# Splitting the operands of the scan's C-times-state product into three fp32r matmuls

## The chip, the cores and the metric

The kernel runs as one program on one core of a Trainium2 chip. The metric is device time in microseconds (us) of one execution, as the median of several runs; lower is better. The core's engines have queues of their own and run side by side: PE multiplies matrices, DVE, ACT and POOL do elementwise work, and DMA transfers are issued from the queues of SP and ACT. On every queue the instructions go in order: an instruction that waits holds back all that stand behind it.

## The reference, cut to what matters

One layer of an encoder with 1024 tokens and a width of 1024. Its input projection feeds a windowed attention branch and a state-space (SSD) branch, which are merged; a cross-attention and an MLP with 4096 hidden columns follow. The change lies in the SSD branch: 8 groups of 4 heads, a state of 128 rows per head column, 8 chunks of 128 tokens, and a scan in both directions.

```python
CB = jnp.einsum('bclgn,bcsgn->bcgls', Cc, Bc)
Wd = CB[:, :, :, None] * segsum_exp(adt)
y_diag = jnp.einsum('bcgrls,bcsgrp->bclgrp', Wd, xdt)
states = jnp.einsum('bcsgn,bcgrs,bcsgrp->bcgrpn', Bc, decay_states, xdt)
...
_, prev = lax.scan(step, init, (jnp.moveaxis(states, 1, 0), jnp.moveaxis(chunk_decay, 1, 0)))
y_off = jnp.einsum('bclgn,bcgrpn,bcgrl->bclgrp', Cc, prev, jnp.exp(a_cs))
...
y = y_fwd + y_bwd + d_skip.astype(f32)[:, None] * xs
y = y.reshape(b, l, D_INNER) * jax.nn.silu(z.astype(f32))
yg = yg * lax.rsqrt(jnp.mean(yg * yg, axis=-1, keepdims=True) + EPS)
```

All inputs and outputs are fp32.

## The kernel before, in words

Most matrix products are made from split operands: a high part `hi` that is the fp32 value copied to the type fp32r, and a low part `lo`, which is the value minus `hi`. `mm3` then issues three fp32r matmuls (hi by hi, hi by lo, lo by hi) into one accumulator. Splitting takes one copy on ACT and one subtraction on POOL (for weights, `split_in`, lines 64 and 67) or on DVE. The scan itself has some products in plain fp32.

`ssd_phase` is a list of jobs. For each group there is a job for each of four convolved inputs (`conv_job`, named `cps` in the profile), one for a block of gate logits (`gate_job`, `gps`) and one for z (`z_job`, `zp`). A job yields after each unit of three matmuls, and `at` says after which unit a piece of scan work is put in. PE runs in exactly this written order. For the other engines a scheduler sets the order of each queue when the program is built. The order of a group is: `conv_job` 0 and 1, `gate_job`, `conv_job` 2 and 3, `z_job`. The scan steps of the group before go into the first four of these, two to a job (after units 8 and 16), from chunk 7 down to 0; in each job a unit is three matmuls of 512 columns. The last group's steps go into three more gate jobs, closer together.

The names to follow:

- `state(q, c)`, in the z job, makes the states of chunk c in three fp32r products (`st`, lines 551 to 553) and puts the running states into `prev` (128 by 8 chunks by 2 directions by 256).
- `back(q, c)` on POOL adds the backward direction's decayed state into `prev`.
- `prep(q, c)` loads two rows of cumulated decay by DMA (`rows`, issued on ACT's queue, line 573), masks them on POOL (lines 574 and 576) and takes their exponentials on ACT, one for each of four heads and two directions (`ef`, `eb`, lines 583 and 584); DVE adds the two (line 585).
- `mask(q, c)` makes the product of C and B (`cb`, line 590), with which DVE multiplies `ef` (line 592).
- `step(q, c)` makes the in-chunk product (`cb`, line 606, four heads of 64 columns) and the product of C with the states (`yo`, line 610, plain fp32, 512 columns, or 256 for chunks 0 and 7). DVE scales `yo` into `t` (line 614), POOL makes the skip term `p1` and adds the backward half to it (lines 621, 623), and DVE adds up `y` and multiplies it by the gate factors `zs` (lines 628 to 630). ACT squares it and sums it (line 631). After every fourth chunk `scale_rows` takes the inverse root on POOL (`rr`, line 122) and scales the four rows on ACT (line 642); `yt` turns them on PE and stores them.
- A `conv_post` follows each convolution job: ACT reads the accumulator (line 413), DVE adds four shifted products (lines 417 and 419), ACT takes a tanh (`th`, line 421), DVE finishes (line 422).

Buffers come from named rings: `wop` has 6 buffers of weights, which is three pairs; `raw` 2; `rows` 2; `ef` 3. The z job uses two pairs of weights: one from `wop` and one in tiles of its own, `z0` and `z1`.

Of the kernel before, what the change touches and what calls it, by code (L numbers as in the profile page):

```python
# [7 lines left out]
F32 = mybir.dt.float32  # L8
F32R = mybir.dt.float32r
I32 = mybir.dt.int32  # L10
AF = mybir.ActivationFunctionType
ALU = mybir.AluOpType
# [4 lines left out]
P = 128  # L17
S = 1024
D = 1024
NT = 8  # L20
# [37 lines left out]
def split_in(kx, src, hi, lo, eng=None, pin=False):  # L58

    nc = kx.nc  # L60
    n = hi.shape[-1]
    raw = kx.wp.tile([P, 1024], F32, tag="raw", bufs=kx.raw_bufs, name="raw")[:, :n]
    nc.sync.dma_start(raw, src)
    steps = [nc.scalar.activation(hi, raw, AF.Copy)]  # L64
    if pin:
        kx.tc.keep_in_program_order(steps[0])
    steps.append((eng or nc.gpsimd).tensor_tensor(lo, raw, hi.bitcast(F32), ALU.subtract))  # L67
    if pin:
        kx.tc.keep_in_program_order(steps[1])


def wload(kx, src, n=1024, hi=None, lo=None, eng=None, pin=False):
    if hi is None:
        hi = kx.wp.tile([P, 1024], F32R, tag="wop", bufs=6, name="whi")[:, :n]
        lo = kx.wp.tile([P, 1024], F32R, tag="wop", bufs=6, name="wlo")[:, :n]
    split_in(kx, src, hi, lo, eng, pin)
    return hi, lo
# [372 lines left out]
def ssd_phase(kx, ins, dr):  # L450


    nc, tc = kx.nc, kx.tc
    V, A, G, PE = nc.vector, nc.scalar, nc.gpsimd, nc.tensor
    with tc.tile_pool(name="p1", bufs=1) as sp, tc.manual_schedule(engines={mybir.EngineType.PE}):
# [31 lines left out]

        def z_job(q):
            def load():
                zhl = [sp.tile([P, 1024], F32R, tag=f"z{i}", bufs=1, name=f"z{i}") for i in range(2)]  # L490
                return [wload(kx, ins["wssd"][q.g, 4], hi=zhl[0], lo=zhl[1]), wload(kx, ins["wssd"][q.g, 5])]

            def run(zw):
                zws = wsplit(zw[0], 4) + wsplit(zw[1], 4)
                q.zt = []
                q.zs = sp.tile([P, NT, 256], F32, tag="zs", bufs=1, name="zs")
                for b in range(3, -1, -1):
                    zp = kx.pp.tile([P, 512], F32, tag="p", name="zp")
                    for j in range(2):
                        t = 2 * b + j  # L500
                        for k in range(NK):
                            mm3(kx, zp[:, j * 256:(j + 1) * 256],
                                act_pair(kx.hT[t // 4], k, slice((t % 4) * P, (t % 4) * P + P)),
                                zws[k], k == 0, k == NK - 1)
                            yield
                    zb = q.zs[:, 2 * b:2 * b + 2].rearrange("p c q -> p (c q)")
                    q.zt.append(A.activation(zb, zp, AF.Tanh, scale=0.5))
                    V.scalar_tensor_tensor(zb, zb, 1.0, zp, ALU.add, ALU.mult)
            return load, run
# [77 lines left out]
        def mask(q, c):  # L587
# [3 lines left out]
            ef = q.efs[c]  # L591
            V.tensor_tensor(ef, ef, cb[:, :P].unsqueeze(1).broadcast_to([P, 4, P]), ALU.mult)

        def step(q, c):

            b, j = c // 4, c % 4
            cl = slice(c * P, (c + 1) * P)
            cb, ef = q.cb, q.efs[c]
            if c:
                mask(q, c - 1)  # L600
            if c > 1:
                prep(q, c - 2)
            if j == 3:
                q.yz, q.ss = [None] * 4, sp.tile([P, 4], F32, tag="ss", bufs=2, name="ss")
            for h in range(4):
                PE.matmul(cb[:, 256 + 64 * h:256 + 64 * h + 64], ef[:, h], q.xtok[:, c, 64 * h:64 * h + 64],  # L606
                          start=True, stop=True)
            lo, hi = (256 if c == 0 else 0), (256 if c == NT - 1 else 512)
            yo = kx.pp.tile([P, 512], F32, tag="p", name="yo")
            PE.matmul(yo[:, lo:hi], q.CT[:, cl], q.prev[:, c].rearrange("p d q -> p (d q)")[:, lo:hi],  # L610
                      start=True, stop=True)
            d0, d1 = lo // 256, hi // 256
            t = sp.tile([P, 2, 256], F32, tag="t", bufs=1, name="t")
            V.tensor_tensor(t[:, d0:d1].rearrange("p d (h q) -> p d h q", h=4),
                            yo[:, lo:hi].rearrange("p (d h q) -> p d h q", h=4, q=64),
                            kx.ecs[:, b, j, d0:d1, q.hs].unsqueeze(3).broadcast_to([P, d1 - d0, 4, 64]), ALU.mult)
            single = q.g == NG - 1 and b == 0
            if single and j == 0:
                scale_rows(q, 1, 3)
            p1 = sp.tile([P, 256], F32, tag="p1", bufs=2, name="p1")  # L620
            G.tensor_tensor(heads(p1), heads(q.xtok[:, c]), dsk[:, q.hs].unsqueeze(2).broadcast_to([P, 4, 64]), ALU.mult)
            if d1 - d0 == 2:
                G.tensor_tensor(p1, p1, t[:, 1], ALU.add)
            if c > 1:
                with tc.issue_after(q.shut.ins):
                    back(q, c - 1)
            y = q.yz[j] = sp.tile([P, 256], F32, tag="yz", bufs=8, name="yz")
            V.tensor_tensor(y, cb[:, 256:], t[:, d0], ALU.add)
            V.tensor_tensor(y, y, p1, ALU.add)
            V.tensor_tensor(y, y, q.zs[:, c], ALU.mult)  # L630
            A.activation(q.zs[:, c], y, AF.Square, accum_out=q.ss[:, j:j + 1])
            if single and j == 0:
                scale_rows(q, 0, 1)
                q.done = b, q.yz
            elif not single and j == 0:
                scale_rows(q, 0, 4)
                q.done = b, q.yz
# [21 lines left out]
        for g in range(NG):  # L659
            q, o = gs[g], gs[g - 1]  # L660
            scan = lambda *cs: [(step, o, c) for c in cs] if g else []
            if g == 0:
                job(conv_job(q, 3), {8: [(tm_x, q)]})
            else:
                job(conv_job(q, 0), {8: [(step, o, 7)], 16: [(step, o, 6)]})
                job(conv_job(q, 1), {8: [(step, o, 5)], 16: [(step, o, 4)]})
                job(gate_job(g), {8: [(step, o, 3)], 16: [(step, o, 2)]})
                job(conv_job(q, 2), {8: [(step, o, 1)], 16: [(yt, o), (step, o, 0)]})
                job(conv_job(q, 3), {8: [(tm_x, q)], 16: [(yt, o)]})
            first = 17 if g else 24  # L670
            at = {first + (63 - first) * c // 7: [(state, q, c)] for c in range(NT)}
            at[4] = [(tm_b, q)]
            at.setdefault(58, []).append((prep, q, 7))
            at[64] = [(prep, q, 6), (mask, q, 7)]
            job(z_job(q), at)
        q = gs[7]
        job(gate_job(8), {5: [(step, q, 7)], 10: [(step, q, 6)], 15: [(step, q, 5)]})
# [3 lines left out]
        for n, ((_, run), at) in enumerate(jobs):  # L681
            nxt = jobs[n + 1][0][0]() if n + 1 < len(jobs) else None
            i = 0
# [1206 lines left out]
```

## Time and profile before

| | us |
|---|---|
| median of 3 runs | 2308.64 (2307.11 to 2309.57) |
| the profiled execution, its own time | 2306.48 |
| its span, first to last instruction | 2304.7 |
| PE busy | 2288.2 (99%) |
| DVE busy | 1582.1 (69%) |
| ACT busy | 1173.3 (51%) |
| POOL busy | 935.3 (41%) |
| the SSD phase with scan steps, from about 126 to 900: PE busy of 774 | 772.6 |

Rows of the profile give the source line, the engine, the operation, the tile written and the tiles read. Matmul durations in the groups contain the way through the array, and overlap; the chain of waits shows how long each holds PE. Times are from the start of the span. The 774 us of the scan hold 7 periods of about 101.8 us, one for each group, that look alike; the period whose steps start at 655 us serves as the example.

### The profile page before, as it was taken

How to read it: one execution, taken by the hardware profiler on the slowest of the kernel's cores; microseconds unless marked ns; L12 is line 12 of the kernel's file. 1: busy time of each engine (PE TensorE's matmuls, PEld its weight loads, DVE VectorE, ACT ScalarE, POOL GpSimd, SP SyncE). 2: the span in 40 equal slices, each digit the busy share in tenths (PEclk: the TensorE clock that was granted, in tenths of full speed). 3: DMA queues.
4: the chain of work that ended last, by engine and by line, in shares of the span. 5: the costliest groups of instructions: out<-in, count | busy, mean ns of one | idle time of the engine just before them, and what ended most of it. 6: DMA issues, size and time to landing. Idle time of an engine off the chain costs nothing.

```text
span 2304.7 us, 32485 instructions
## 1 busy us (share of the span) xinstructions
PE 2288.2 (99%) x11882; PEld 1941.3 (84%) x11882; DVE 1582.1 (69%) x2501; ACT 1173.3 (51%) x2486; POOL 935.3 (41%) x885
## 2 busy tenths in 40 slices
PE   9999999999999999999999999999999999999998
PEld 8888898989888897888888888888988887888887
DVE  5877666677766673467659887866685456489984
ACT  5454655555565555488865442346563334233341
POOL 2355647555564745355540021125585454100010
PEclk9999999999999999999999999999999999999999
DMA  6222323233232323111145257112453345712201
GB/s 235 83 83 92 110 74 110 83 101 91 93 102 74 119 74 110 40 44 35 51 153 183 92 184 255 45 37 65 138 177 129 118 152 183 274 74 108 103 28 74
DMA packets 150754, 252.09 MB, mean 109 GB/s; under 512 B 11457, under 2 KB 86337, under 8 KB 150594
## 3 DMA queue, kind: packets, MB, share of 16 engines
q1 hardware_dynamic: 79840, 211.46, 27.1%
q10 hardware_dynamic: 70754, 38.55, 5.9%
q8 instruction: 94, 1.54, 0.3%
q14 instruction: 66, 0.54, 0.1%
HBM read 202.25 MB, written 47.71 MB: 108 GB/s over the span
## 4 chain that ended last, share of the span: by engine, by line
PE 88%; DVE 4%; ACT 2%; DMA 2%; issue 1%; POOL 1%; ACTq 0%; SPq 0%; POOLq 0%; DVEq 0%
PE mps L1630 10%; PE dps L1630 10%; PE pb L1416 6%; PE cps L83 4%; PE cps L88 4%; PE cps L87 4%; PE pc L1416 3%; PE zp L83 2%; PE zp L88 2%; PE zp L87 2%; PE cb L606 2%; PE yo L610 2%; PE gps L83 2%; PE gps L88 2%; PE gps L87 2%; PE mps L87 1%
## 5 line engine op out<-in xcount | busy, mean ns | idle before, releaser
L67 POOL TENSOR_TENSOR wlo<-raw,whi 128x1024 fp32r<-128x1024 f32 x96 | 235.5, 2453 | 385.3 <-ACT whi L64 374.1
L1581 ACT ACTIVATE kt<-row 128x512 fp32r<-128x512 f32 x264 | 143.8, 619 | 183.6 <-PE dps L1630 82.9
L1630 PE MATMUL mps<-kt 128*128 128x512 f32 x1008 | 229.8, 389 | 0.0
L1630 PE MATMUL dps<-kt 128*128 128x512 f32 x1008 | 228.6, 389 | 0.0
L1630 PEld LDWEIGHTS dps<-kt 128*128 128x128 f32 x1008 | 189.2, 188 | 39.3
L1630 PEld LDWEIGHTS mps<-kt 128*128 128x128 f32 x1008 | 188.9, 188 | 39.4 <-DVE kt L1582 0.3
L83 PE MATMUL cps<-kt,whi 128*128 128x512 f32 x512 | 215.2, 420 | 0.0
L88 PE MATMUL cps<-kt,wlo 128*128 128x512 f32 x512 | 200.0, 391 | 0.0
L87 PE MATMUL cps<-kt,whi 128*128 128x512 f32 x512 | 199.3, 389 | 0.0
L64 ACT ACTIVATE whi<-raw 128x1024 fp32r<-128x1024 f32 x104 | 109.6, 1055 | 149.1 <-DMA raw<-in_wa_dram 27.4
L1582 DVE TENSOR_TENSOR kt<-row,kt 128x512 fp32r<-128x512 f32 x264 | 171.5, 697 | 1.5 <-ACT kt L1581 1.4
L548 POOL TENSOR_TENSOR xl<-xs,xh 128x512 fp32r<-128x512 f32 (+1 forms) x64 | 85.9, 1343 | 105.4 <-ACT xh L547 80.7
L122 POOL TENSOR_TENSOR rr<-rv,mhalf 128x1 f32<-128x1 f32 (+2 forms) x50 | 34.6, 694 | 226.1 <-DVE rv L120 224.3
L1361 POOL TENSOR_TENSOR wop<-w,wop 128x512 fp32r<-128x512 f32 x64 | 87.1, 1363 | 82.6 <-ACT wop L1360 79.1
L87 PEld LDWEIGHTS cps<-kt,whi 128*128 128x128 f32 x512 | 96.3, 188 | 25.3 <-issue 6.7
L83 PEld LDWEIGHTS cps<-kt,whi 128*128 128x128 f32 x512 | 96.2, 188 | 24.9 <-issue 5.5
L88 PEld LDWEIGHTS cps<-kt,wlo 128*128 128x128 f32 x512 | 96.1, 188 | 20.8
L583 ACT ACTIVATE ef<-rows,ebias 128x128 f32<-128x128 f32 x256 | 91.2, 394 | 34.4 <-PE cb L606 30.8
L808 DVE CUSTOM_DVE_ANT_0 t<-sps,bias,snk 128x384 f32<-128x384 f32 (+1 forms) x128 | 71.4, 581 | 52.3 <-PE sps L807 51.7
L816 POOL TENSOR_SCALAR t<-t,den 128x384 f32<-128x384 f32 (+1 forms) x128 | 69.2, 560 | 90.3 <-DVE den L814 81.2
L584 ACT ACTIVATE eb<-rows,ebias 128x128 f32<-128x128 f32 x256 | 89.9, 394 | 30.2 <-POOL rows L576 30.1
L1299 POOL TENSOR_TENSOR wd<-row,wd 128x1024 fp32r<-128x1024 f32 x4 | 11.1, 2794 | 228.4 <-ACT wd L1298 228.4
(392 smaller groups left out, 6576.7 us busy)
## 6 DMA issues: line engine op xcount, KB each, us to landing
rows<-d_cs ACTq DMA_DIRECT2D x128, 256.0 KB, 3.8
raw<-in_wssd_dram SPq DMA_DIRECT2D x48, 512.0 KB, 3.8
raw<-in_wup_dram SPq DMA_DIRECT2D x41, 512.0 KB, 4.2
d_u<-c SPq DMA_DIRECT2D x64, 256.0 KB, 3.0
row<-in_wdn_dram SPq DMA_DIRECT2D x28, 512.0 KB, 6.4
row<-d_u SPq DMA_DIRECT2D x28, 512.0 KB, 6.2
x<-in_x_dram SPq DMA_DIRECT2D x16, 512.0 KB, 6.6
raw<-in_wg_dram SPq DMA_DIRECT2D x16, 512.0 KB, 3.7
```

Source lines behind the costliest of these rows:

```text
L64: steps = [nc.scalar.activation(hi, raw, AF.Copy)]
L67: steps.append((eng or nc.gpsimd).tensor_tensor(lo, raw, hi.bitcast(F32), ALU.subtract))
L83: i = mm(out, l[0], r[0], start=first, stop=False)
L87: mm(out, l[0], r[1], start=False, stop=False)
L88: mm(out, l[1], r[0], start=False, stop=last)
L583: A.activation(ef[:, h], rows[:, 0, h], AF.Exp, bias=kx.ebias[:, b, j, 0, o:o + 1])
L584: A.activation(eb[:, h], rows[:, 1, h], AF.Exp, bias=kx.ebias[:, b, j, 1, o:o + 1])
L1361: self.kx.nc.gpsimd.tensor_tensor(t[:, 1], src, t[:, 0].bitcast(F32), ALU.subtract)
L1416: self.kx.nc.tensor.matmul(ps, w[:, i, ks], act[:, k, j], start=start and k == 0 and m == 0, stop=k == 3 and m == 2, skip_group_check=True)
L1581: nc.scalar.activation(t[:, j, 0], src, AF.Copy)
L1582: nc.vector.tensor_tensor(t[:, j, 1], src, t[:, j, 0].bitcast(F32), ALU.subtract)
L1630: self.kx.nc.tensor.matmul(ps[t], lt[:, k, x, ts], rt[:, k, y], start=n in (1, 2, 5) and k == 0 and m == 0, stop=k == 3 and m == 2, skip_g ...
```

## The change

1. `step` makes `yo` from three fp32r products of split operands in the place of one fp32 product. C is split once for each group (`split_c`: one ACT copy, one DVE subtraction of 128x1024, after unit 52 of the z job). The states of a chunk are split just before they are used (`split_prev`: one ACT copy to `prh`, one DVE subtraction to `prl`, 128x512, or 128x256 for chunks 0 and 7). The pair has one buffer. The split for chunk c-1 is written into step c, behind the scaling of `yo`, and the block `issue_after` puts the subtraction behind that scaling in DVE's queue; it adds no wait to ACT's copy.
2. The product with the gate factors is written over them (`zs[:, c]`), and the squares go to `y`, which now has 2 buffers; the 8 buffers of `yz` are gone.
3. The z job takes both pairs of weights from the common ring `wop`, which still has three pairs; `z0` and `z1` are gone.

```diff
         def z_job(q):
             def load():
-                zhl = [sp.tile([P, 1024], F32R, tag=f"z{i}", bufs=1, name=f"z{i}") for i in range(2)]
-                return [wload(kx, ins["wssd"][q.g, 4], hi=zhl[0], lo=zhl[1]), wload(kx, ins["wssd"][q.g, 5])]
+                return [wload(kx, ins["wssd"][q.g, i]) for i in (4, 5)]
...
+        def split_c(q):
+            q.chl = [sp.tile([P, S], F32R, tag=n, bufs=1, name=n) for n in ("ch", "cl")]
+            A.activation(q.chl[0], q.CT, AF.Copy)
+            V.tensor_tensor(q.chl[1], q.CT, q.chl[0].bitcast(F32), ALU.subtract)
+
+        def split_prev(q, c):
+            lo, hi = (256 if c == 0 else 0), (256 if c == NT - 1 else 512)
+            q.pair = [sp.tile([P, 512], F32R, tag=n, bufs=1, name=n) for n in ("prh", "prl")]
+            ph, pl = (t[:, lo:hi] for t in q.pair)
+            pv = q.prev[:, c].rearrange("p d q -> p (d q)")[:, lo:hi]
+            A.activation(ph, pv, AF.Copy)
+            V.tensor_tensor(pl, pv, ph.bitcast(F32), ALU.subtract)
...
-            PE.matmul(yo[:, lo:hi], q.CT[:, cl], q.prev[:, c].rearrange("p d q -> p (d q)")[:, lo:hi],
-                      start=True, stop=True)
+            ph, pl = (t[:, lo:hi] for t in q.pair)
+            PE.matmul(yo[:, lo:hi], q.chl[0][:, cl], pl, start=True, stop=False)
+            PE.matmul(yo[:, lo:hi], q.chl[0][:, cl], ph, start=False, stop=False)
+            PE.matmul(yo[:, lo:hi], q.chl[1][:, cl], ph, start=False, stop=True)
...
+            if c:
+                with tc.issue_after(scaled.ins):
+                    split_prev(q, c - 1)
...
-            y = q.yz[j] = sp.tile([P, 256], F32, tag="yz", bufs=8, name="yz")
+            y = sp.tile([P, 256], F32, tag="y", bufs=2, name="y")
+            yz = q.yz[j] = q.zs[:, c]
...
-            V.tensor_tensor(y, y, q.zs[:, c], ALU.mult)
-            A.activation(q.zs[:, c], y, AF.Square, accum_out=q.ss[:, j:j + 1])
+            V.tensor_tensor(yz, y, yz, ALU.mult)
+            A.activation(y, yz, AF.Square, accum_out=q.ss[:, j:j + 1])
...
+            at.setdefault(52, []).append((split_c, q))
...
-            at[64] = [(prep, q, 6), (mask, q, 7)]
+            at[64] = [(prep, q, 6), (mask, q, 7), (split_prev, q, 7)]
```

The line numbers of the changed kernel are shifted by up to 19 behind the new functions. The next rows are instructions in the order of their queues.

PE, one step of 512 columns between two jobs, before:

```order
L590 MATMUL cb<-cC,cB 128x128
L606 MATMUL cb<-xtok,ef 128x64 x4
L610 MATMUL yo<-prev,cC 128x512
L83 MATMUL cps<-kt,whi 128x512
L87 MATMUL cps<-kt,whi 128x512
```

PE, the same place in the changed kernel:

```order
L589 MATMUL cb<-cC,cB 128x128
L618 MATMUL cb<-xtok,ef 128x64 x4
L623 MATMUL yo<-prl,ch 128x512
L624 MATMUL yo<-prh,ch 128x512
L625 MATMUL yo<-prh,cl 128x512
```

One fp32 matmul became three fp32r ones, and the first of them reads the low part `prl`, which DVE writes last.

ACT, from the reading of the second convolution job's accumulator to the scaling of the first four rows, before. The numbers at the names tell buffers apart: `ef_5977` and `ef_6044` belong to chunks 1 and 0, `rows_6609` to chunk 7 of the next group, `yz_5912` to chunk 4, `rr_5919` is the inverse root of chunks 7 to 4:

```order
L413 ACTIVATE cx_5925<-cps_5784,cols_376 128x1024
L583 ACTIVATE ef_5977<-rows_5968,ebias_175 128x128 x4
L584 ACTIVATE eb_6045<-rows_6035,ebias_175 128x128 x4
L64 ACTIVATE whi_6079<-raw_6081 128x1024
L573 DMA rows_6609<-d_cs_72 128x4x128 x2
L583 ACTIVATE ef_6044<-rows_6035,ebias_175 128x128 x2
L421 ACTIVATE th_5931<-cx_5925 128x1024
L631 ACTIVATE zs_5265,ss_5684<-yz_5912 128x256
L583 ACTIVATE ef_6044<-rows_6035,ebias_175 128x128 x2
L573 DMA rows_6658<-d_cs_72 128x4x128
L642 ACTIVATE yz_5912<-yz_5912,rr_5919 128x256
```

ACT, the same place in the changed kernel. `prh_6142` and `prh_6239` are the high parts of chunks 3 and 2, `ef_6217` and `ef_6290` the exponentials of chunks 1 and 0, `rr_6159` the inverse root of chunks 7 to 4:

```order
L413 ACTIVATE cx_6165<-cps_6012,cols_376 128x1024
L603 ACTIVATE prh_6142<-prev_5503 128x512
L582 ACTIVATE ef_6217<-rows_6208,ebias_175 128x128 x4
L583 ACTIVATE eb_6291<-rows_6281,ebias_175 128x128 x4
L572 DMA rows_6873<-d_cs_72 128x4x128 x2
L649 ACTIVATE y_6152,ss_5900<-zs_5473 128x256
L582 ACTIVATE ef_6290<-rows_6281,ebias_175 128x128 x3
L660 ACTIVATE zs_5473<-zs_5473,rr_6159 128x256 x4
L421 ACTIVATE th_6171<-cx_6165 128x1024
L603 ACTIVATE prh_6239<-prev_5503 128x512
```

The scaling of the four rows, which waits for `rr` from POOL, now stands ahead of the tanh, and the split of chunk 2 behind both.

DVE, the end of the second convolution job's sums, before (`t_5995` is chunk 3's scaled product):

```order
L419 SCALAR_TENSOR_TENSOR cx_5925<-cps_5784,cols_376,cx_5925 128x1022
L630 TENSOR_TENSOR yz_5912<-yz_5912,zs_5265 128x256
L592 TENSOR_TENSOR ef_5887<-ef_5887,cb_5965 128x512
L585 TENSOR_TENSOR ef_5977<-ef_5977,eb_5978 128x512
L422 SCALAR_TENSOR_TENSOR cx_5925<-th_5931,cx_5925 128x1024
L120 TENSOR_SCALAR rv_5917<-ss_5684 128x4
L614 TENSOR_TENSOR t_5995<-yo_5993,ecs_176 128x512
```

DVE, the same place in the changed kernel (`t_6237` is chunk 3's scaled product, `prl_6240` the low part of chunk 2):

```order
L120 TENSOR_SCALAR rv_6157<-ss_5900 128x4
L591 TENSOR_TENSOR ef_6121<-ef_6121,cb_6205 128x512
L419 SCALAR_TENSOR_TENSOR cx_6165<-cps_6012,cols_376,cx_6165 128x1022
L584 TENSOR_TENSOR ef_6217<-ef_6217,eb_6218 128x512
L628 TENSOR_TENSOR t_6237<-yo_6233,ecs_176 128x512
L646 TENSOR_TENSOR y_6249<-cb_6109,t_6237 128x256
L422 SCALAR_TENSOR_TENSOR cx_6165<-th_6171,cx_6165 128x1024
L604 TENSOR_TENSOR prl_6240<-prev_5503,prh_6239 128x512
```

The sum for the inverse root (`rv`) went ahead of the job's last step (L422), and the low part of chunk 2 stands right behind that step.

POOL, the same place in the changed kernel (`wlo_6332` is a weight's low part, `p1_6146` the skip term of chunk 4):

```order
L573 AFFINE_SELECT rows_6281<-rows_6281 128x512
L67 TENSOR_TENSOR wlo_6332<-raw_6333,whi_6331 128x1024
L575 AFFINE_SELECT rows_6281<-rows_6281 128x512
L640 TENSOR_TENSOR p1_6146<-p1_6146,t_6140 128x256
L564 TENSOR_TENSOR cb_t_6318<-prev_5503,dec_177 128x256
L565 TENSOR_TENSOR prev_5503<-prev_5503,cb_t_6318 128x256
L638 TENSOR_TENSOR p1_6315<-xtok_5393,dsk_944 128x256
L573 AFFINE_SELECT rows_6873<-rows_6873 128x512
L122 TENSOR_TENSOR rr_6159<-rv_6157,mhalf_169 128x4
```

The inverse root has one masking of rows for the next group ahead of it; before, both stood ahead of it.

More of the change, by code (lines that the diff above doesn't have):

```diff
@@ L609, in step @@
             yo = kx.pp.tile([P, 512], F32, tag="p", name="yo")
-            PE.matmul(yo[:, lo:hi], q.CT[:, cl], q.prev[:, c].rearrange("p d q -> p (d q)")[:, lo:hi],
-                      start=True, stop=True)
+            ph, pl = (t[:, lo:hi] for t in q.pair)
+            PE.matmul(yo[:, lo:hi], q.chl[0][:, cl], pl, start=True, stop=False)
+            PE.matmul(yo[:, lo:hi], q.chl[0][:, cl], ph, start=False, stop=False)
+            PE.matmul(yo[:, lo:hi], q.chl[1][:, cl], ph, start=False, stop=True)
             d0, d1 = lo // 256, hi // 256
             t = sp.tile([P, 2, 256], F32, tag="t", bufs=1, name="t")
-            V.tensor_tensor(t[:, d0:d1].rearrange("p d (h q) -> p d h q", h=4),
+            scaled = V.tensor_tensor(t[:, d0:d1].rearrange("p d (h q) -> p d h q", h=4),
                             yo[:, lo:hi].rearrange("p (d h q) -> p d h q", h=4, q=64),
                             kx.ecs[:, b, j, d0:d1, q.hs].unsqueeze(3).broadcast_to([P, d1 - d0, 4, 64]), ALU.mult)
+            if c:
+                with tc.issue_after(scaled.ins):
+                    split_prev(q, c - 1)
             single = q.g == NG - 1 and b == 0
```

## The prediction

> **What bounds the kernel now.** I read the page first: busy shares and the chain of work that ended last.
>
> ```profile
> span 2304.7 us, 32485 instructions
> PE 2288.2 (99%) x11882; PEld 1941.3 (84%) x11882; DVE 1582.1 (69%) x2501; ACT 1173.3 (51%) x2486; POOL 935.3 (41%) x885
> PE 88%; DVE 4%; ACT 2%; DMA 2%; issue 1%; POOL 1%; ACTq 0%; SPq 0%; POOLq 0%; DVEq 0%
> ```
>
> PE is the bound: time taken off its queue comes off the end, as long as PE does not wait instead. Next the stretch in which the scan steps run, and in it four successive intervals, each from the end of one `yo` to the end of the next.
>
> ```profile
> 126.00:900.00 774.00, 772.62 (x4480) 667.39 (x4479) 531.63 (x740) 436.53 (x1054) 459.47 (x459) 1.00 0.31 95
> 671.48:678.92 7.44, 7.44 (x38) 6.00 (x37) 7.15 (x10) 4.46 (x11) 5.13 (x7) 1.00 0.45 135
> 678.92:686.36 7.44, 7.44 (x38) 6.00 (x37) 6.33 (x9) 5.59 (x14) 7.04 (x8) 1.00 0.33 102
> 686.36:693.80 7.44, 7.44 (x38) 6.00 (x37) 7.13 (x10) 3.05 (x8) 5.98 (x6) 1.00 0.51 160
> 693.80:701.24 7.44, 7.44 (x38) 6.00 (x37) 3.71 (x8) 3.48 (x9) 5.78 (x6) 1.00 0.48 161
> ```
>
> After each stretch and its length the columns are busy us of PE, weight load, DVE, ACT and POOL. PE waits 1.4 us in all of 774, at a granted clock of 1.00. But DVE is nearly full in the two convolution jobs: 7.15, 6.33 and 7.13 of 7.44, and rests only in the gate job (3.71). That is where a new dependency can turn into a wait.
>
> **The matmuls.** The chain of waits shows what a product holds PE for.
>
> ```profile
> 656.11 0.49 PE yo L610 x2
> 670.57 0.91 PE yo L610 x2
> 692.89 0.91 PE yo L610 x2
> 729.44 0.12 PE st L551
> 731.93 0.23 PE st L551
> 732.16 0.23 PE st L552
> 732.40 0.24 PE st L553
> ```
>
> The fp32 `yo` takes 0.91 us with 512 columns and 0.49 with 256. The states' own fp32r products, three into one accumulator as the changed `yo` will have them, take 0.23 + 0.23 + 0.24 = 0.70 and 3 x 0.12 = 0.36. A step thus saves 0.21 or 0.13. A group has 6 wide and 2 narrow steps: 6 x 0.21 + 2 x 0.13 = 1.52 us; 8 groups give **12.2 us**. No row shows three fp32r products right behind the fp32 `cb`; the 0.69 that three times 0.23 gives would add 0.5 us in all, and I leave it out.
>
> **The splits.** ACT gets 64 copies and 8 of C, DVE as many subtractions. By the nearest rows (ACT's copy of 128x512 and DVE's subtraction to fp32r of that size):
>
> ```profile
> L547 ACT ACTIVATE xh<-xs 128x512 fp32r<-128x512 f32 x6 | 3.8, 628 | 2.6 <-PE zp L88 1.1 <-PE st L552 0.9 <-DVE xs L543 0.6
> L520 DVE TENSOR_TENSOR bl<-tm,bh 128x512 fp32r<-128x512 f32 x2 | 1.3, 674 | 0.0
> L543 DVE TENSOR_TENSOR xs<-xtok,coef 128x512 f32<-128x512 f32 x6 | 7.8, 1297 | 1.8 <-POOL xl L548 1.8
> ```
>
> a wide split is 0.63 on ACT and 0.67 on DVE, up to the 1.30 that DVE's product of two SBUF tiles has in the z job. By themselves they are hidden: PE reads the pair a whole step later. C's split (about twice that, 1.3 and 1.3 us) lies in the z job, 12 units of 3 x 0.12 and 8 of 3 x 0.23 us ahead of the first step, some 10 us; it costs nothing while PE has these matmuls. Its low bound is nothing, its high one 1 us a group, if it holds up a state's split. But DVE gets fuller: the three intervals from 671.48 hold 7.15 + 6.33 + 7.13 = 20.61 us of work, with three subtractions 22.6, in 3 x 7.23 = 21.7 us. The queue falls behind by about 1 us by chunk 2's step and catches up in the gate job. So the question is which step's `prl` comes too late.
>
> **The wait that can come.** The order of the changed queues shows it at one place in each of the seven first groups: chunk 2's pair stands, on ACT, behind the scaling of four rows (which waits for POOL's inverse root) and the tanh, and on DVE behind L422. I follow that chain from the end of chunk 5's `yo`, with rows of the same kind:
>
> ```profile
> L421 ACT ACTIVATE th<-cx 128x1024 f32<-128x1024 f32 x2 | 2.1, 1062 | 3.0 <-DVE cx L419 3.0
> L574 POOL TENSOR_SCALAR_AFFINE_SELECT rows<-rows 128x512 f32<-128x512 f32 x9 | 6.1, 677 | 6.7 <-DMA rows<-d_cs 6.2 <-ACT ef L583 0.3 <-ACT yz L642 0.2
> L576 POOL TENSOR_SCALAR_AFFINE_SELECT rows<-rows 128x512 f32<-128x512 f32 x8 | 5.5, 693 | 3.5 <-DMA rows<-d_cs 3.5
> L67 POOL TENSOR_TENSOR wlo<-raw,whi 128x1024 fp32r<-128x1024 f32 x6 | 14.4, 2401 | 6.0 <-ACT whi L64 6.0
> L122 POOL TENSOR_TENSOR rr<-rv,mhalf 128x4 f32<-128x4 f32 x2 | 2.0, 1012 | 4.4 <-DVE rv L120 4.4
> L422 DVE SCALAR_TENSOR_TENSOR cx<-th,cx 128x1024 f32<-128x1024 f32 x2 | 3.4, 1704 | 0.0
> 675.32 0.39 ACT L584 ACTIVATE eb<-rows,ebias 128x128 f32<-128x128 f32 x1
> 675.45 0.37 ACTq L573 DMA_DIRECT2D rows<-d_cs  x1
> 675.61 0.39 ACT L584 ACTIVATE eb<-rows,ebias 128x128 f32<-128x128 f32 x1
> 881.91 1.70 ACT L642 ACTIVATE yz<-yz,rr 128x256 f32<-128x256 f32 x4 [1.56 <-POOL rr L122]
> DMA to landing us min/median/max: 3.5/3.9/4.3
> DMA to landing us min/median/max: 4.9/5.0/5.2
> DMA to landing us min/median/max: 3.2/3.4/3.6
> DMA to landing us min/median/max: 5.1/5.3/5.4
> ```
>
> The last four rows are the two `rows` transfers of one `prep` each: at 675.4 and 683.5 (the two places that count here), and at 776.1 and 377.8, the same places in other groups. A transfer is issued 0.13 us after the first exponential ahead of it starts (675.32, 675.45).
> - ACT: split of chunk 4 0.63, an exponential 0.39, tanh 1.06, two exponentials 0.78, then the first `eb` of chunk 1 and the issue of chunk 0's rows 0.13: 2.99.
> - The transfer's first half lands after 3.5: 6.5. POOL masks 0.68, splits a weight 2.40, masks 0.69: 10.3.
> - ACT starts `eb` of chunk 0 and issues the next group's rows, 0.13; they land after 4.9: 15.3.
> - POOL masks 0.68 and takes the root 1.01; ACT scales four rows 1.70, tanh 1.06; DVE finishes L422 1.70 and subtracts 0.67: 22.1.
> - Instructions that follow each other on an engine overlap by 0.39 - (675.61 - 675.32) = 0.10; there are eight such handovers: **21.3 us**.
>
> Due it is at the start of chunk 2's `yo`: before, 692.89 - (670.57 + 0.91) = 21.41 later, now two `yo` less 0.21 each: 20.99. It is late by 0.3 us, a wait of PE of **0.3 us in each of 7 groups, 2.1 us**. With the shortest of the four landings at both places (3.2) the chain is 19.3 us, and there is no wait; with the longest (5.1) it is 23.1, a wait of 2.1 us a group, 14.7 in all. I take 0.3, since it comes from the rows of these very places. A late step is made good behind it: in the gate job DVE has 3.7 us free in a step.
>
> At the other steps I find room. Chunk 4's pair stands behind L422 too, but with no root ahead of its tanh: 0.63 + 0.39 + 1.06 + 1.70 + 0.67 = 4.5 us from the same start, due after 7.23 - 0.70 = 6.5. Chunk 3's has neither tanh nor root ahead of it. In the last group, with steps closer together, chunk 5's subtraction stands behind an add that waits for POOL:
>
> ```profile
> 866.24 0.43 DVE L629 TENSOR_TENSOR yz<-yz,p 128x256 f32<-128x256 f32 x1 [1.54 <-POOL p L623]
> 867.83 1.08 PE L610 MATMUL yo<-prev,cC 128*128 128x512 f32 x2
> ```
>
> 866.24 + 0.43 + 0.67 = 867.3 against a `yo` due near 867.83 - 0.35 = 867.5: 0 to 1 us once, taken as 0.
>
> **The ring and the rows y.** z's first pair now waits for the gate job's weights to be done, and the second convolution job's for z's first pair. Each is then split a job of 16 units, 11 us, ahead of its use, where POOL needs 2.40; I cost them at nothing, with bounds of 0 and, if ACT's copy waits with a state's split behind it, 1 us a group. `zs` is overwritten by the next tanh only after PE's turns of the rows, which stand ahead of z's matmuls on PE: nothing. The squares now go to `y`: same instruction.
>
> **Sum.** The profiled execution took 2306.48: 2306.5 - 12.2 + 2.1 = 2296.4. The median of the runs lies 2.2 us above it, at 2308.64, so I say **2298.5 us**.
>
> **The rivals.** Below 0.2%, 4.6 us, a measurement of this kernel can hardly tell a difference from none.
>
> *No change.* Chunk 2's pair is late by 1.1 to 2.4 us, and the waits eat the saving; at 12.2 / 7 = 1.7 us a group nothing is left (2308.6). For it speaks that two landings of 5.1 already make 2.1, and that DVE has no room in these jobs. Against it, the rows of the very places land after 3.5 and 4.9.
>
> *Slower.* POOL stops the subtraction of chunk 2. A row of DVE shows what that costs:
>
> ```profile
> 859.16 2.50 DVE L629 TENSOR_TENSOR yz<-yz,p 128x256 f32<-128x256 f32 x1
> ```
>
> This add of two SBUF tiles takes 0.43 at 866.24 and here 2.50; POOL splits a weight in 2.40. The new subtraction too reads two SBUF tiles. Behind the root, POOL has one more such weight split in that job; if it starts ahead of the subtraction, this ends 2.4 later, so 0.3 + 2.4 = 2.7 us a group, 18.9 in all: 2306.5 - 12.2 + 18.9 + 2.2 = 2315.4. It decides from 2.4 us a group on. Against it: that weight split stands behind the masking of rows which ACT issues only after chunk 2's copy, so it comes more than 3.2 us behind that copy, when L422 (1.70) and the subtraction should be through. The Trainium skill has a rule for the row (SBUF — State Buffer, "Who interferes with whom"): a DVE instruction with two SBUF inputs contends with a GpSimd instruction that reads SBUF, and whoever issues first has the shared port pair for the whole instruction. The trace agrees by the 2.50 above and by L543's mean of 1.30. By this rule every one of the 64 subtractions can lose up to 2.4 us, but only chunk 2's has no room for it.
>
> *The products are not shorter.* If an fp32r product behind fp32 work held PE for the 0.39 of its record and not 0.23, a wide step would cost 3 x 0.39 = 1.17, which is 0.26 more than now: 48 x 0.26 = 12.5 us slower, 2321. The chain speaks against it: `st` stands among fp32r work, but the first product behind each `yo` also shows 0.23 there.
>
> **How the numbers follow.** The forecast, with waits of up to 1.1 us a group (2296.4 to 2304.0 by the medians), gets 0.73; no change 0.15; the blocked subtraction 0.09; longer products 0.03. That gives faster 0.73, same 0.15, slower 0.12. The range reaches from 2294, with no wait at all and products of 0.69 in sum (2308.6 - 12.7 = 2295.9) and 2 us for the spread of the runs, up to 2309, the middle of no change. The likeliest case alone spans 2295 to 2304.
>
> **What would show it.** In the profile after, the chain shows `yo` as three products of 0.23, and steps of 7.23 in the place of 7.44 wherever PE doesn't wait. PE's waits have a group of `yo` L623 for DVE's `prl`, seven times in chunk 2's step, 0 to 1 us long; if they are over 1.7 us, the saving is gone. If they stand at another chunk, my chain is wrong. `prl` means under 1.0 us; over 1.3 speaks for POOL's stops. What makes the prediction wrong above all is a landing of the rows about 1 us later than here, since it counts twice.

## The result

The changed kernel takes 2332.97 us, median of 4 runs (2330.03 to 2335.38); the kernel before, on the same chip, 2309.11 (2307.11 to 2310.22). The ratio is 1.0106, 95% interval 1.0094 to 1.0117: slower by 1.1%, where 2298.5 was forecast. The profiled execution took 2335.38, against 2306.48 before. The page of the changed kernel begins like this (span; busy time, share and instructions of each engine; shares of the chain that ended last):

```profile
span 2333.2 us, 32783 instructions
PE 2295.3 (98%) x11946; PEld 1960.6 (84%) x11946; DVE 1655.7 (71%) x2573; ACT 1211.6 (52%) x2558; POOL 958.2 (41%) x885
PE 72%; POOL 7%; DMA 6%; DVE 6%; ACT 5%; issue 4%; ACTq 0%; POOLq 0%; SPq 0%; DVEq 0%
```

PE's share of the chain falls from 88% to 72%; DMA and POOL are now on it. The same stretch as before, and two successive intervals from the end of one `yo` to the end of the next (chunk 3's, then chunk 2's; columns as in the prediction):

```profile
126.00:900.00 774.00, 752.56 (x4410) 663.66 (x4410) 580.95 (x778) 457.74 (x1082) 463.58 (x440) 0.99 0.30 91
592.20:599.49 7.29, 7.29 (x39) 6.18 (x37) 5.97 (x10) 4.58 (x12) 6.57 (x7) 1.00 0.26 84
599.49:609.12 9.63, 7.48 (x38) 6.26 (x37) 9.08 (x14) 5.82 (x13) 4.40 (x7) 1.00 0.24 70
```

PE waits 21.4 us there, where it waited 1.4. A step without a wait takes 7.29, chunk 2's 9.63. PE's waits (waiting operation, releaser, us in total, times, the longest):

```profile
PE yo L623 <- DVE prl L604: 20.5, 13, 2.6
PE yt L667 <- ACT zs L660: 2.0, 1, 2.0
```

Seven of the thirteen are chunk 2's, one a group: 1.99, 2.54, 2.55, 2.56, 2.15, 2.61 and 2.42 us, 16.8 in all. Five are chunk 4's (1.16, 0.56, 0.17, 0.21, 0.33, 2.4 in all), and one is in the last group (1.27).

Where the time went is seen from three places of each trace: the first `yo` of all, the last group's first `yo`, and the last turn `yt`; of before first, then of after (start, duration):

```profile
147.09 0.65 PE L610 MATMUL yo<-prev,cC 128*128 128x256 f32 x2
857.46 0.65 PE L610 MATMUL yo<-prev,cC 128*128 128x256 f32 x2
903.29 1.04 PE L649 MATMUL yt<-ident,yz 128*128 128x128 f32 x8
```

```profile
146.85 0.37 PE L623 MATMUL yo<-prl,ch 128*128 128x256 f32 x1
882.35 0.37 PE L623 MATMUL yo<-prl,ch 128*128 128x256 f32 x1
931.35 1.03 PE L667 MATMUL yt<-ident,zs 128*128 128x128 f32 x8
```

Seven groups with the z jobs between them took 710.37 and now take 735.50; the last group 45.83 and now 49.00; all else 1548.5 and 1548.7. So 25.1 us were lost in the seven groups and 3.2 in the last, 28.3 of the 28.9 between the two executions.

The waits alone are too small for that: 19.2 us of them lie in the seven groups, and the products are shorter. Most of the rest is the clock. PE's rows behind one wait, and the windows of 4 us behind three waits of yo (1.99 at 186.40, 2.54 at 292.30 and 1.27 at 893.90) and behind that of `yt` (2.05 at 909.50), with the granted clock as third number from the end:

```profile
292.36 0.66 PE L623 MATMUL yo<-prl,ch 128*128 128x512 f32 x1 [2.54 <-DVE prl L604]
293.68 0.63 PE L83 MATMUL cps<-kt,whi 128*128 128x512 f32 x1
```

```profile
186.40:190.40 4.00, 3.92 (x10) 3.12 (x11) 3.97 (x7) 2.94 (x6) 2.61 (x3) 0.57 0.58 179
292.30:296.30 4.00, 3.94 (x10) 3.12 (x11) 3.97 (x7) 2.93 (x6) 2.69 (x3) 0.57 0.58 179
...
893.90:897.90 4.00, 3.94 (x17) 3.30 (x18) 3.08 (x5) 3.28 (x11) 3.84 (x6) 1.00 0.02 4
909.50:913.50 4.00, 3.82 (x12) 2.91 (x13) 1.82 (x4) 3.80 (x11) 2.89 (x5) 0.60 0.00 0
```

Behind the wait of 2.54 a matmul shows 0.63 and not 0.39, and only 10 or 11 of them fit into 4 us where behind the wait of 1.27 (at 893.90) there are 17. Such a stretch lasts about 3.5 us (0.43 of 4 us lost is 3.4 us at half clock). Six of chunk 2's seven waits have one (clock 0.57 four times, 0.59, 0.63; the wait of 2.15 has none): (4 x 0.43 + 0.41 + 0.37) x 4 = 10.0 us lost, and 0.40 x 4 = 1.6 behind `yt`. This sums up for the seven groups: waits 19.2, clock 10.0, products -7.4 (7 groups of 6 x 0.15 + 2 x 0.08, from the steps 7.44 to 7.29 and 7.01 to 6.93), and 2.3 if the ring and the rows y are taken from the one trace of the first experiment: 24.1 of 25.1. The 2.3 are not shown to be a cost: three executions of one and the same code for these groups, further down, differ by 2.6 us. So some 3 us stay without a name.

### The profile page after: what moved, and what is told of

Read it like the earlier page. It is cut to its first block, busy times and chain, and to the rows that moved or that the text cites. A ratio compares the mean times of both kernels' runs of the same rounds, so it can differ in the third digit from the quotient of the medians.

```text
span 2333.2 us, 32783 instructions
## 1 busy us (share of the span) xinstructions
PE 2295.3 (98%) x11946; PEld 1960.6 (84%) x11946; DVE 1655.7 (71%) x2573; ACT 1211.6 (52%) x2558; POOL 958.2 (41%) x885
## 4 chain that ended last, share of the span: by engine, by line
PE 72%; POOL 7%; DMA 6%; DVE 6%; ACT 5%; issue 4%; ACTq 0%; POOLq 0%; SPq 0%; DVEq 0%
PE mps L1649 10%; PE dps L1649 10%; PE pb L1435 6%; DMA rows<-d_cs 5%; PE pc L1435 3%; PE cps L87 3%; PE cps L83 3%; PE cps L88 3%; POOL wlo L67 2%; PE mps L88 1%; PE mps L83 1%; PE pt L841 1%; PE mps L87 1%; PE pd L1435 1%; POOL rows L575 1%
## 5 line engine op out<-in xcount | busy, mean ns | idle before, releaser
L67 POOL TENSOR_TENSOR wlo<-raw,whi 128x1024 fp32r<-128x1024 f32 x104 | 256.5, 2467 | 370.6 <-ACT whi L64 359.6
L83 PE MATMUL cps<-kt,whi 128*128 128x512 f32 x512 | 204.2, 399 | 0.0
L87 PE MATMUL cps<-kt,whi 128*128 128x512 f32 x512 | 203.2, 397 | 0.0
L64 ACT ACTIVATE whi<-raw 128x1024 fp32r<-128x1024 f32 x112 | 118.2, 1056 | 153.2 <-PE mps L87 34.0
L83 PE MATMUL zp<-whi,kt 128*128 128x256 f32 x512 | 145.9, 285 | 0.0
L87 PE MATMUL zp<-wlo,kt 128*128 128x256 f32 x512 | 144.7, 283 | 0.0
L88 PE MATMUL zp<-whi,kt 128*128 128x256 f32 x512 | 144.7, 283 | 0.0
L88 PEld LDWEIGHTS cps<-kt,wlo 128*128 128x128 f32 x512 | 98.1, 192 | 21.3
```

The lines of the kernel that those rows point to most:

```text
L83: i = mm(out, l[0], r[0], start=first, stop=False)
L87: mm(out, l[0], r[1], start=False, stop=False)
L88: mm(out, l[1], r[0], start=False, stop=last)
```

## The experiments

My theory after these traces: (A) chunk 2's pair is late because it ends a long chain, DVE's arrears make that chain longer, and each wait of PE near 2 us also costs half a clock for 3.5 us. Rivals: (B) the ring, the added load or the products cost by themselves; for the clock, that it has another cause. All medians below are beside runs of before on the same chip.

**One part alone.** Ring and rows without the rest; all splits, but the fp32 product; the products, with one pair a group.

```
ring_only:   before + z_job's load() and y/zs rows of the change
splits_only: changed kernel, step: PE.matmul(yo, CT, prev)  (fp32, as before)
one_pair:    changed kernel, split_prev(q, 6) at unit 64, none in step;
             all steps read that pair
```

> The kernel before with only z's first weight pair in the common ring and the rows y written over the gate factors; the product stays fp32, nothing is split. Theory A (and the prediction): within 1.5 us of before. Theory B (the ring makes weights late): 2312 or more, with PE waiting for whi or wlo.

Measured 2308.14 (before 2307.56; ratio 1.0002, 0.9994 to 1.0011): as A and the prediction had it. In its trace the seven groups take 712.65, 2.3 more than before, which the time of the whole does not show; one trace cannot tell it from the spread.

> The changed kernel with all its splits, ring and rows, but the step's product again the one fp32 product of C with prev; nobody reads the pairs. Theory A (DVE's and ACT's added work only hurts because yo waits for its end): 2309, within 2 us of before, though DVE has some 60 us more to do. Theory B (the added work delays masks, evictions or states and so PE by itself): 2314 or more, with waits of PE for DVE or ACT at other products.

Measured 2312.47 (1.0025, 1.0014 to 1.0036): between the two theories. Its seven groups take 712.37, no more than with the ring alone, so in this trace splits that nobody waits for cost nothing there. Its last group takes 49.73 instead of 46.43: `yt` waits 3.0 us for ACT's scaled rows, and the clock of 868 to 894 is 0.93. In the last group B holds.

> The changed kernel, but every group splits chunk 6's states alone and all eight steps multiply C with that pair; the other 56 splits are left out (so the product with C is not that of the reference). No step can wait for a split. Theory A (the loss is the waits for chunk 2's pair and the half clock behind them, and the products themselves are 0.15 us shorter a wide step and about 0.10 a narrow one): 48 x 0.15 + 16 x 0.10 = 8.8 us below before, about 2300, no wait of yo for prl, clock 1.00. The prediction's own sizes (0.21 and 0.13) would give 2297. Theory B (the three products or the common ring of weights hold PE by themselves): 2306 or more, with waits or longer matmuls elsewhere.

Measured 2304.66 (0.9990, 0.9981 to 0.9999), between the two theories. The seven groups take 704.60, that is 5.8 less than before and 8.1 less than with the ring alone, so the products do save; but this row of its waits is the last group's, and that group takes 50.20, 4.4 more than before:

```profile
PE yt L664 <- ACT zs L657: 3.8, 1, 3.8
```

So without any late split the whole kernel gains 2.9 us, not 12.2.

**The clock.** Eight or four idle products are put where PE stood.

```
+ if c == 2 and q.g < NG - 1:
+     for _ in range(8):        # fill4: range(4)
+         PE.matmul(yo, q.chl[0][:, cl], q.chl[0][:, 0:512], start=True, stop=True)
```

> The changed kernel with eight more fp32r products of 512 columns ahead of yo of chunk 2, in the first seven groups; they read only C's split and write into yo, which the step's own products then overwrite. They take 8 x 0.23 = 1.9 us of the time in which PE waited 2.0 to 2.6 us. Theory A (the clock is halved because PE stood still): chunk 2's pair comes at the same time, the rest of the wait is 0 to 0.8 us, no stretch at half clock follows, and the time falls by about 10 us, to 2321 to 2325, although PE has 13 us more work. Theory B (the half clock has another cause): no gain, 2333 or more.

> As with eight filling products ahead of chunk 2's yo, but four, 0.9 us: PE then stands still for 1.1 to 1.7 us there instead of 2.0 to 2.6. Theory A (a standstill must be near 2 us to halve the clock): no or few stretches at half clock, 2323 to 2327 as with eight. Theory B (any standstill over 1 us does it): stretches at half clock in six groups as in the changed kernel, 2331 or more.

Measured 2324.93 (1.0077, 1.0064 to 1.0091) with eight, 2324.24 (1.0073, 1.0059 to 1.0086) with four: 0.3% faster than the changed kernel by the ratios to before (some 7 us; 8 to 9 by the medians, which come from different chips), with more work on the engine that is the bound. First with eight, then with four: the filling products and `yo` of chunk 2 in the second group, and the 4 us behind them:

```profile
288.25 2.10 PE L624 MATMUL yo<-ch 128*128 128x512 f32 x8
290.73 0.50 PE L626 MATMUL yo<-prl,ch 128*128 128x512 f32 x1 [0.38 <-DVE prl L604]
291.00:295.00 4.00, 4.00 (x19) 3.24 (x19) 3.13 (x6) 2.69 (x6) 2.99 (x3) 1.00 0.60 187
```

```profile
289.90 0.50 PE L626 MATMUL yo<-prl,ch 128*128 128x512 f32 x1 [0.95 <-DVE prl L604]
291.00:295.00 4.00, 4.00 (x19) 3.30 (x18) 3.13 (x4) 2.00 (x5) 2.78 (x3) 1.00 0.64 215
```

The 2.54 us of standstill became 0.38 and 0.95, and the clock stays 1.00 with 19 matmuls instead of 10. In the seven groups no stretch at half clock is left in either kernel, with waits up to 1.51. These groups take 724.12 and 723.49 us, where the changed kernel's took 735.50. Theory A holds: the halved clock follows PE's standstill, and about 10 us of the loss are that.

**The chain to chunk 2's pair.** Root and scaling taken from ahead of it; and DVE relieved ahead of it.

```
late_scale: c == 4: q.late = q.yz, q.ss          (instead of scale_rows)
            c == 3: with tc.issue_after(<chunk 2's copy>): scale_rows(...)
short_lo:   subtraction of chunks 5, 4, 3 over pl[:, :64] only
```

> The changed kernel, but in the first seven groups the root and the scaling of the first four rows are issued behind chunk 2's copy on ACT, so neither stands ahead of chunk 2's pair any more; its subtraction now also stands ahead of L422 on DVE. Buffers and products are the same. Theory A (chunk 2's pair is late because it ends a chain through POOL's root, ACT's scaling and the tanh): the wait falls from 2.0 to 2.6 us to 0 to 0.5 us, no half clock follows, and the time falls by 20 to 25 us, to 2308 to 2313. Theory B (it is late because DVE is behind with its work, wherever the pair stands): the wait falls by under 1 us and the time stays over 2320.

> The changed kernel, but DVE's subtractions for chunks 5, 4 and 3 cover 64 columns instead of 512 (the other columns keep an older chunk's low parts, so these steps' products are not the reference's). Copies on ACT, waits and order stay. DVE has about 3 x 0.9 = 2.7 us less to do ahead of chunk 2's pair in each of the first seven groups. Theory A (DVE's arrears delay the ACT and POOL steps of the chain to chunk 2's pair): the wait there falls from 2.4 to 0.5 to 1.5 us and the time to 2312 to 2322. Theory B (the chain runs through landings, ACT and POOL alone): the wait falls by under 0.4 us, and the time stays over 2327.

Waits of yo for prl, first of the kernel with the late scaling, then of the one with the short subtractions:

```profile
PE yo L623 <- DVE prl L604: 4.7, 10, 0.9
```

```profile
PE yo L625 <- DVE prl L606: 15.1, 12, 2.4
```

The late scaling gives 2309.08 (1.0004, 0.9995 to 1.0013): nearly all 24 us are back, with the same pair buffers, splits and products. Its waits are single ones of 0.3 to 0.9. So it was what stood ahead of the pair. But the edit moved more than the root and the scaling: in the same step the copy on ACT (587.18) now also runs ahead of the tanh (588.87), and the subtraction on DVE (589.96) ahead of L422 (590.55). What the root, the scaling, the tanh and L422 give each alone is not shown. The short subtractions give 2322.34 (1.0064, 1.0051 to 1.0076), just above the range that A gave, and the wait fits neither theory: chunk 2's waits fall from 2.4 to 1.9 us on average (2.41, 1.33, 2.07, 1.80, 2.45, 1.18, 1.75), where A said 0.5 to 1.5. Half clocks fall from six to three. So these three subtractions carry about 0.5 of the 2.4 us; in this trace the root waits 0.29 us for the sums `rv` that DVE hands over in its own late turn. What of the rest DVE's other work carries is not settled by it. These waits also show that it isn't length alone that halves the clock; PE's row and the window behind it for two of them:

```profile
601.80 0.47 PE L625 MATMUL yo<-prl,ch 128*128 128x512 f32 x1 [2.45 <-DVE prl L606]
808.12 0.66 PE L625 MATMUL yo<-prl,ch 128*128 128x512 f32 x1 [1.75 <-DVE prl L606]
```

```profile
601.80:605.80 4.00, 4.00 (x18) 3.28 (x19) 2.41 (x5) 2.95 (x6) 1.46 (x3) 1.00 0.83 263
808.12:812.12 4.00, 4.00 (x11) 3.13 (x12) 2.50 (x5) 2.94 (x6) 1.66 (x3) 0.57 0.82 259
```

**Can the saving be kept?** Two buffers for the pair, and the split a step earlier; then variants of it.

```
early:          prh, prl with bufs=2; step: back(q, c - 1); split_prev(q, c - 2)
early_yt:       early + gate job 9: (yt, q) at unit 16 instead of 12, step 2 ahead of it
late_scale_yt:  late_scale + the same
early_yt_first: early_yt, the three products of yo ahead of both cb
early7:         early, but the last group keeps the fp32 product, no splits
early_short:    early, every subtraction over 64 columns
early_pool:     early, subtraction by nc.gpsimd
```

> The changed kernel with two buffers for the pair, so that the split of a chunk is issued a step earlier, as soon as its states are complete, and no longer behind the step before it. Theory A (only the late pair and the half clock behind it cost): no wait of yo for prl, clock 1.00, and the time of the kernel with one pair a group plus at most 2 us for the other splits: 2304 to 2307, that is 0.1 to 0.2% below before or the same. Theory B (DVE and ACT's added work holds PE elsewhere): 2310 or more. By the prediction's 12.2 us it would be 2297.

Measured 2307.95 (0.9999, 0.9990 to 1.0008), just above the range that A gave. No wait for prl is left, and the seven groups take 707.71. The last takes 48.58: `yt` waits 2.9 us.

> The kernel with two buffers for the pair and the earlier split, and in the last group PE's turns of the first four rows three units of matmuls and one step later (unit 16 of the gate job instead of 12), so that ACT's scaling is done by then. Theory A (the 2.9 us that PE stands there, and the half clock behind it, some 1.7 us, are lost time): 2303 to 2305, 0.1 to 0.2% below before. Theory B (the wait only moves to the next product): 2307 to 2309 as without the move.

> The kernel with the root and scaling behind chunk 2's copy (one buffer for the pair), and the last group's turns at unit 16 as well. Theory A: 3 to 3.5 us below the kernel without the moved turns, 2305 to 2306. Theory B (the wait only moves): 2308 to 2310.

Measured 2310.59 (1.0011, 1.0002 to 1.0020) and 2310.74 (1.0013, 1.0004 to 1.0021): 2 to 3 us slower for the move, just above what B said: as in B, the wait only moves. With the turns put later, the first kernel shows this row in the last group; in the second, yo waits 4.4 us for prl there.

```profile
889.48 0.70 PE L665 MATMUL yt<-ident,zs 128*128 128x128 f32 x4 [4.87 <-DVE t L628]
```

> As the kernel with the moved turns, but the three products of yo stand ahead of the step's fp32 products cb, right behind the convolution's fp32r products. Theory A (the 0.06 us more of the first product is the price of any change from fp32 to fp32r on PE, and before it lay in the 0.91 us of the fp32 product's place): it moves to the first convolution product behind cb, steps stay 7.29, time the same within 1 us. Theory B (it is the first product's own): steps of 7.23, 48 x 0.06 = 2.9 us less.

Measured 2308.40 (1.0003, 0.9994 to 1.0012), 2.2 us below the kernel without this order, whose waits differ too (4.9 + 2.6 there, 3.3 + 2.1 here). The steps decide: 565.29 - 557.99 = 7.30 between two starts of yo, as before the move. The chain of waits shows where the 0.06 is now:

```profile
558.15 0.23 PE yo L614
...
559.06 0.84 PE cb L624 x8
559.90 0.28 PE cps L83
```

It goes with whatever stands behind the short `cb`, as A said.

> The kernel with two buffers for the pair and the earlier split, but the last group, whose steps follow each other every 5.25 us, keeps the fp32 product and splits nothing. Theory A (seven groups save 0.98 us of products each, and what is given back lies mostly in the last group: 2.9 us of standstill and 1.7 us of half clock): 2302 to 2305, 0.1 to 0.25% below before. Theory B (the added work costs as much in every group): 2307 to 2309.

Measured 2308.36 (0.9998, 0.9989 to 1.0007): no gain, B. The last group is nearly back (46.53), but the seven groups, of the same code as above, take 710.32 in this execution and not 707.71. Waits of yo for t are 3.4 us in this trace and 1.4 in that one. The longest of them; PE's row of chunk 2's yo, and DVE's of chunk 3's t:

```profile
286.18 0.50 PE L624 MATMUL yo<-prl,ch 128*128 128x512 f32 x1 [1.36 <-DVE t L632]
```

```profile
285.45 0.68 DVE L632 TENSOR_TENSOR t<-yo,ecs 128x512 f32<-128x512 f32 x1
```

Chunk 3's products were done near 278.0, DVE reads them at 285.45, and chunk 2's yo, which has its pair, waits for that accumulator.

> The kernel with two buffers for the pair and the earlier split, but every subtraction covers 64 columns, and the first product reads these 64 repeated (the low parts of the other columns are left out, so the product with C is not the reference's). Copies on ACT, product lengths and order stay; DVE has 62 x about 0.9 = 55 us less to do. Theory A (what the two-buffer kernel gives back lies on DVE, which reads t of chunk 3 so late that yo of chunk 2 waits for its accumulator, and in the last group): no wait of yo for t, 2303 to 2305, close to the kernel with one pair a group (2304.7). Theory B (it lies in ACT's copies or in the ring of weights): 2307 to 2309.

> The kernel with two buffers for the pair and the earlier split, with the subtraction on POOL instead of DVE (complete, same values). POOL needs about 1.3 us for one, has 41% of the span busy, but also writes the masks and the root. Theory A (DVE's arrears are what is left): 2303 to 2306. Theory B (POOL's own chain of masks, root and p1 becomes the late one): waits of yo for prl on POOL or of yt for ACT's scaling, 2309 or more.

With short subtractions 2307.35 (0.9998, 0.9989 to 1.0007): missed as a whole, and yet it tells the causes apart. The seven groups take 704.46, as with one pair a group (704.60), and no yo waits there: so in these traces the 3 to 6 us between this and the kernels with whole subtractions (707.71, 708.74, 710.32 in three executions) are DVE's. The last group takes 50.30, with one wait of 2.4 us for DVE's t and half a clock behind it.

With the subtraction on POOL 2332.79 (1.0110, 1.0094 to 1.0125): POOL needs 1420 ns for one of 512 columns, its masks come late, and PE now waits for DVE's masked factors:

```profile
PE cb L618 <- DVE ef L591: 13.5, 8, 2.5
```

Only the kernel that leaves out 56 splits has an interval below 1; no complete version beats the kernel before.

## Why the prediction was wrong

**The place was right, the wait's size was the step that failed.** One late pair a group, chunk 2's, in seven groups, behind the chain that the prediction follows: the late scaling shows that it is what stands ahead of the pair. I gave the wait 0.3 us; it is 2.4 on average, 16.8 us instead of 2.1 in all. Here is the chain as it ran in one group, from the end of chunk 5's yo at 584.68 (its record starts at 583.74, and the chain of waits ends such a yo 0.94 later); ACT, POOL, DVE and PE in one order of time, each row from its engine's timeline:

```profile
585.56 0.42 ACT L649 ACTIVATE y<-zs 128x256 f32<-128x256 f32 x1 [1.19 <-DVE zs L648]
588.57 0.37 ACTq L572 DMA_DIRECT2D rows<-d_cs  x1
592.84 0.85 POOL L638 TENSOR_TENSOR p<-xtok,dsk 128x256 f32<-128x256 f32 x1 [0.96 <-DVE y L647]
593.65 0.63 POOL L573 TENSOR_SCALAR_AFFINE_SELECT rows<-rows 128x512 f32<-128x512 f32 x1
594.26 2.41 POOL L67 TENSOR_TENSOR wlo<-raw,whi 128x1024 fp32r<-128x1024 f32 x1
597.81 0.37 ACTq L572 DMA_DIRECT2D rows<-d_cs  x1
602.04 0.64 POOL L573 TENSOR_SCALAR_AFFINE_SELECT rows<-rows 128x512 f32<-128x512 f32 x1 [1.60 <-DMA rows<-d_cs]
603.69 1.71 ACT L660 ACTIVATE zs<-zs,rr 128x256 f32<-128x256 f32 x4 [1.48 <-POOL rr L122]
606.38 1.23 DVE L422 SCALAR_TENSOR_TENSOR cx<-th,cx 128x1024 f32<-128x1024 f32 x1 [0.52 <-ACT th L421]
607.52 0.68 DVE L604 TENSOR_TENSOR prl<-prev,prh 128x512 fp32r<-128x512 f32 x1
608.35 0.47 PE L623 MATMUL yo<-prl,ch 128*128 128x512 f32 x1 [2.15 <-DVE prl L604]
```

The same times in the kernel before, counted from 671.48, stand in the middle:

| us after the end of chunk 5's yo | predicted | kernel before | changed kernel |
| --- | --- | --- | --- |
| rows issued | 3.0 | 4.0 (675.45) | 3.9 (588.57) |
| POOL starts the mask | 6.5 | 8.3 (679.80) | 9.0 (593.65) |
| next rows issued | 10.4 | 12.0 (683.50) | 13.1 (597.81) |
| POOL masks them | 15.3 | 17.5 (688.96) | 17.4 (602.04) |
| subtraction done, overlaps taken off | 21.3 | | 23.5 (608.20) |

The 2.2 us are there by the second line, and both times an engine waits for DVE: ACT for the row product that its Square reads, POOL for the y that frees p1. Most of this lateness stood in the kernel before, where nothing of PE hung on it: the prediction names the issues at 675.4 and 683.5, but adds up durations to 3.0 and 10.4 instead of taking 4.0 and 12.0. The landing, which I named as the main risk, was shorter than taken: 602.04 - 597.81 = 4.2, not 4.9.

**What I misread is DVE.** I added its work in three intervals, found it 1 us over, and took its queue to be on time at the start. It was not, in the kernel before already:

```profile
676.59 0.68 DVE L614 TENSOR_TENSOR t<-yo,ecs 128x512 f32<-128x512 f32 x1
691.70 0.68 DVE L614 TENSOR_TENSOR t<-yo,ecs 128x512 f32<-128x512 f32 x1
```

Chunk 5's yo ended at 670.57 + 0.91 = 671.48 and was read 5.1 us later, chunk 3's ended at 685.45 + 0.91 = 686.36 and was read 5.3 later. Nothing of PE waited for that, so no view of waits told it. In the changed kernel it was 3.2 and 5.1 us (587.90 and 604.73), so the added work did not make it worse at these two places. How much of the 2.2 us is DVE's stays open beyond the 0.5 of the short subtractions. The subtractions were also longer than the 0.67 taken: the 48 wide ones take 1.24 on average, just under the bound of 1.30. This row mixes the 16 narrow ones in:

```profile
L604 DVE TENSOR_TENSOR prl<-prev,prh 128x512 fp32r<-128x512 f32 (+1 forms) x64 | 67.6, 1056 | 10.0 <-ACT prh L603 9.9
```

**The clock was not in the sum at all.** 11.6 us. I had a bound of 14.7 us for the waits, close to the 16.8 of chunk 2, but priced a wait by its length; a wait near 2 us costs up to 1.7 more. The prediction's own sign, over 1.7 us a group and the saving is gone, held.

**The products.** I took 0.70 and 0.36 and left out what no row showed, three fp32r products behind fp32 cb. It is the term that was mis-sized:

```profile
614.99 0.84 PE cb L618 x8
615.83 0.29 PE yo L623
616.12 0.23 PE yo L624
616.35 0.23 PE yo L625
```

0.75 and not 0.70: a wide step saves 0.15 by the steps, a narrow one 0.08, a group 1.06, all eight 8.5 us instead of 12.2.

**Other chunks.** Room was forecast at chunk 4: five groups wait there, 2.4 us. For the last group I had 0 to 1 us at chunk 5; it was 1.27 for prl and 2.05 for `yt` (0.70 before), whose scaled rows I hadn't costed.

**Ring and rows** cost nothing in the time of the whole, as said.

**The rivals.** "No change" had the right mechanism with waits up to 2.4 us, yet its break-even of 1.7 lay inside that, and without the clock it still came out too low. "Slower" had the sign but another mechanism: chunk 2's subtraction wasn't stopped by POOL in any of the seven groups (0.68 or 0.69). Chunk 1's was, in six of them: 2.59 to 2.73, the longest from 189.60 on, while POOL splits a weight from 189.39 for 2.39. No yo waited for those. The Trainium skill's rule (SBUF — State Buffer, "Who interferes with whom") agrees with that and with the mean of 1.24, but these stops do not decide here.

Against the 2296.4 that was summed for the profiled execution (2335.38), the 39.0 us are: chunk 2's waits 16.8 - 2.1 = 14.7, clock 11.6, products 12.2 - 8.5 = 3.7, the last group 1.27 + 2.05 - 0.70 = 2.6, chunk 4 2.4: together 35.0. If the 2.3 of the ring's one trace are counted, 1.7 are left open, without them 4.0.

## What to carry to other kernels

Before work is put into an engine's queue, compare when its instructions start with when their inputs were ready: an engine that is 70% busy can still be 5 us behind, and what waits for its results inherits that. Where a chain's instructions already run in the kernel before, take their start times from its trace instead of adding up durations. Price a standstill of a bound PE near 2 us at its length plus the half clock behind it, and look for what stands ahead of the late operand (here a root, a scaling and the steps behind them, which could go behind it) before adding buffers. A term that no row shows, such as a product behind another format, belongs into the bounds on both sides.

## What the hardware showed

Short standstills of PE halve its clock for about 3.5 us, in the one case of 3.79 for about 7 (clock 0.50 from 878 to 884 in the kernel with one pair a group). I count the waits between 125 and 960 us in all sixteen traces. Those up to 1.58 us never did it. From 1.60 to 2.47 most did (1.60, 1.75 twice, 1.77 twice, 1.80, 1.95, 1.99, 2.05, 2.37, 2.41, 2.42, 2.47) and some did not (1.74, 2.07, 2.15, 2.23, 2.45). Those of 2.54 to 4.87 did, but for one of 3.29, in the kernel with yo ahead of both cb; a matmul behind it shows 0.40 and not 0.63:

```profile
886.22 0.66 PE L665 MATMUL yt<-ident,zs 128*128 128x128 f32 x4 [3.29 <-DVE t L628]
886.96 0.40 PE L87 MATMUL gps<-kt,whi 128*128 128x512 f32 x1
```

The Trainium skill (TensorE: Matmul & The Clock Gate, "Part 1: The HAM clock gate") tells of a free-running activity window of about 3.4 us, and of throttling after an idle one. The length of the half clock agrees, and so does that a longer wait can pass where a shorter one doesn't; that 1.60 us can do it does not agree with an idle window of 3.4. A shorter free-running idle window does not fit these waits either: it could be at most 1.60 us long, as that wait would have to hold one, and would have to be over 1.64, as two of them must not fit into 3.29. The margin is small, and what decides stays open.
